# Low parts of the split tokens in the up products: a negated copy and an adding transfer instead of a subtraction

## The chip, the cores and the metric

The kernel runs on one core of one Trainium2 chip. The metric is the device time of one execution in microseconds. The kernel before was timed in three runs: 2589.78, 2593.25 and 2595.57 us, median 2593.25 us.

## The reference, cut to what matters

A hybrid decoder of two layers is stepped once, for a prompt of 1024 tokens and for 8 sample tokens, which the kernel treats together as 1032 tokens of width 1024. The whole is in float32.

```python
def hybrid_layer(x, ...):
    n = rms_norm(x, g_mix)
    z = jnp.einsum('bsd,de->bse', n, w_in)          # q | k | v | conformer input
    ...                                              # dilated attention, causal convolution
    h = x + jnp.einsum('bse,ed->bsd', jnp.concatenate([att, cv], axis=-1), w_o)
    n2 = rms_norm(h, g_ffn)
    f = jnp.square(jax.nn.relu(jnp.einsum('bsd,df->bsf', n2, w_up)))   # 1024 -> 4096
    y = h + jnp.einsum('bsf,fd->bsd', f, w_down)                       # 4096 -> 1024
    return y, new_kv, new_conv
```

The change concerns the product of n2 with w_up, once in each layer.

## The kernel before, in words

Tokens lie along the free dimension, features on the 128 partitions. The normalised activations of the MLP are eight tiles x[0] to x[7], each 128 x 1032. The token axis is cut into two halves of TH = 516.

**Exact products from rounded operands.** TensorE takes operands of type fp32r. To keep the accuracy of float32, each operand is split in two: a high part `h`, which is the value copied by ScalarE to an fp32r tile, and a low part `lo`, the rest, which is the value minus `h`. A product is then three matmuls: weight high by token high, weight high by token low, weight low by token high (lines 966 to 968). Weights are split by `split_piece` (ScalarE line 195, VectorE line 196), tokens of the up products by `split_tokens` (ScalarE line 901, VectorE line 902) and, for the operand t2, by lines 915 and 916.

**Seven products in place of eight.** Both MLP products use a Strassen-like scheme with blocks of 2 x 2. With four k-tiles each, b11 is the first token half of x[0..3], b12 their second half, b21 the first half of x[4..7], b22 their second half. The token operands of the seven products are b21, b11, t2 = b22 - (b12 - b11), t1 = b12 - b11, t3 = b22 - b12, b22 and t4 = b21 - t2. The sums are formed by VectorE in place: b11 is overwritten by t1 (line 909), b12 by t3 (line 921), b21 by t4 (line 918). t2 needs a staging tile of 128 x 1032 for each half of its k-tiles (line 914). The staging tile comes from the pool tag "big", which has three buffers; x[6] and x[7] hold two of them. So the second t2 tile needs the buffer of the first.

The products run in the order a12*b21, a11*b11, s2*t2, s1*t1, s3*t3, s4*b22, a22*t4 (`PRODUCTS`), for each of eight groups of 512 hidden features. `group` loads the weight blocks, forms the weight sums s1 to s4 (line 944), splits them, multiplies and drains. The first product is drained by ScalarE into a new tile f11 (line 995), the second is added into f11 by VectorE (line 991). f11 comes from the pool tag "act", which has six buffers, and in the first group these hold x[0] to x[5]. So the first drain needs an x tile that nobody reads any more. The third product accumulates in the PSUM bank that line 991 reads, and the fourth needs the bank that line 995 reads. The finished hidden tiles are stored to DRAM by GpSimd's queue (line 1017).

**Where the change sits.** Before the up products, `ffn_norm` normalises the output of w_o in two token halves. For each half it stores x to DRAM by GpSimd's queue (line 275), squares it on ScalarE (line 280, into one of two buffers of the tag "out"), adds up the squares on VectorE (line 281), sums over partitions on TensorE (line 306), forms the reciprocal root (line 312 on VectorE, 313 on ScalarE, then three Newton steps, lines 288 to 290), broadcasts it by TensorE (line 319) and ScalarE (line 320) and multiplies (line 284). While the second half is normalised, the first half is already split into b21 and b11.

**What sets the order.** The instructions of each engine run in a fixed order. It is decided when the program is built: a planner models the timeline and lets each engine take, among the instructions whose operands and buffers are ready in its model, the one of highest priority. Priority is program order, except in `later(...)`, which moves a block: loads, sums and splits of the up weights are placed 420 instructions earlier. Waits between engines are put in by the builder, and a buffer is handed on when all its readers are done.

Of the kernel before, what the change touches and what calls it, by code (L numbers as in the profile page):

```python
# [7 lines left out]
F32 = mybir.dt.float32  # L8
F32R = mybir.dt.float32r
AF = mybir.ActivationFunctionType  # L10
ALU = mybir.AluOpType
# [63 lines left out]
def tile_hybrid_decoder_step(  # L75
# [20 lines left out]
    nc = tc.nc  # L96
# [119 lines left out]
    for l in range(DEPTH):  # L216
        for b in range(NB):
            for kv in range(2):
                for g, (win, _) in enumerate(GROUPS):
                    n = (win - 1) * 256  # L220
                    src = caches[g][l, b, kv].rearrange("t h d -> (t h d)")
# [4 lines left out]
                    for q in range(parts):  # L226
                        o = q * rows * step
# [4 lines left out]
    def prow(l, what, j):  # L232
        base = {"mix": 0, "ffn": 8, "cb": 16, "lg": 22, "lb": 28}[what]
        return prm[:, NC_L * l + base + j:NC_L * l + base + j + 1]

    def big(name, dt=F32):
        return tp.tile([P, TOK], dt, tag="big", name=name, bufs=3)
# [9 lines left out]
    def norm_split(xk, gcol, nm, by_chunks=False):  # L247

        xh, xl, acc = [], [], None
        for k in range(KD):  # L250
            x = xk(k)
            h = xs.tile([P, TOK], F32R, tag="xh", name=f"xh{nm}_{k}", bufs=8)
            lo = xs.tile([P, TOK], F32R, tag="xl", name=f"xl{nm}_{k}", bufs=8)
            for a, b in ((0, CHUNKS[1][0]), (CHUNKS[1][0], TOK)) if k == 0 and by_chunks else ((0, TOK),):
                nc.scalar.activation(h[:, a:b], x[:, a:b], AF.Copy, scale=gcol(k))
                nc.vector.scalar_tensor_tensor(lo[:, a:b], x[:, a:b], gcol(k), h[:, a:b].bitcast(F32), op0=ALU.mult, op1=ALU.subtract)  # L256
            xh.append(h)
            xl.append(lo)
            if acc is None:
                acc = tp.tile([P, TOK], F32, tag="acc", name=f"acc{nm}", bufs=1)  # L260
            with later(NORM_LATER):
                if k == 0:
                    nc.scalar.activation(acc, x, AF.Square)
                else:
                    sq = spare(f"sq{nm}_{k}")
                    nc.scalar.activation(sq, x, AF.Square)
                    if k < KD - 1:
                        nc.vector.tensor_tensor(acc, acc, sq, op=ALU.add)
        return xh, xl, acc, sq
# [60 lines left out]
    def layer(l, x_first, x_dram, xin, x_last):  # L330
# [540 lines left out]
        with ExitStack() as pb:  # L871
# [11 lines left out]
            def parts_of(op, name):  # L883

                out = []
                for i in range(2):
                    if op in ("b21", "b11", "t2", "t1"):
                        hl = [xs.tile([P, TOK], F32R, tag=t, name=f"{op}{t}{name}{i}", bufs=8) for t in ("xh", "xl")]
                    else:
                        hl = [bp.tile([P, TOK], F32R, tag=t, name=f"{op}{t}{name}{i}", bufs=6) for t in ("oh", "ol")]  # L890
                    out.append(tuple(t.rearrange("p (k t) -> p k t", k=2) for t in hl))
                return out


            ops = {}

            def split_tokens(op, src):
                o = ops[op] = parts_of(op, f"U{nm}")
                for i in range(4):
                    h, lo_t = (t[:, i % 2, :] for t in o[i // 2])  # L900
                    nc.scalar.activation(h, src(i), AF.Copy)
                    nc.vector.tensor_tensor(lo_t, src(i), h.bitcast(F32), op=ALU.subtract)

            b11, b12 = (lambda i: x[i][:, 0:TH]), (lambda i: x[i][:, TH:])
            b21, b22 = (lambda i: x[4 + i][:, 0:TH]), (lambda i: x[4 + i][:, TH:])
            split_tokens("b21", b21)
            split_tokens("b11", b11)
            for i in range(4):
                nc.vector.tensor_tensor(b11(i), b12(i), b11(i), op=ALU.subtract)
            o = ops["t2"] = parts_of("t2", f"U{nm}")  # L910
            for i in range(2):
                t2 = big(f"t2{nm}_{i}").rearrange("p (k t) -> p k t", k=2)
                for j in range(2):
                    nc.vector.tensor_tensor(t2[:, j, :], b22(2 * i + j), b11(2 * i + j), op=ALU.subtract)
                nc.scalar.activation(o[i][0], t2, AF.Copy)
                nc.vector.tensor_tensor(o[i][1], t2, o[i][0].bitcast(F32), op=ALU.subtract)
                for j in range(2):
                    nc.vector.tensor_tensor(b21(2 * i + j), b21(2 * i + j), t2[:, j, :], op=ALU.subtract)
            split_tokens("t1", b11)
            for i in range(4):  # L920
                nc.vector.tensor_tensor(b12(i), b22(i), b12(i), op=ALU.subtract)
# [103 lines left out]
            for c in range(NG // 2):  # L1025
                ops.clear()
                for _, op in PRODUCTS:
                    o = ops[op] = parts_of(op, f"D{nm}_{c}")
                    for i in range(2):
                        h, lo_t = o[i]  # L1030
# [85 lines left out]
    h, lo, acc, sq = norm_split(first, lambda k: prow(0, "mix", k), "m0", True)  # L1116
# [23 lines left out]
    for l in range(DEPTH):  # L1140
        src = (lambda k: xT[:, k, :]) if l == 0 else (lambda k: x_scr[:, k, :])
        xin = layer(l, None, src, xin, between(l) if l < DEPTH - 1 else finish)
# [102 lines left out]
```

## Time and profile before

| | us |
|---|---|
| median of the three runs | 2593.25 |
| the profiled execution | 2595.12 |
| its span, first to last instruction | 2593.3 |
| TensorE (PE) busy | 2477.9 (96%) |
| VectorE (DVE) busy | 1919.5 (74%) |
| ScalarE (ACT) busy | 1080.7 (42%) |
| GpSimd (POOL) busy | 251.3 (10%) |

The mean granted TensorE clock of the execution is 0.977 of full speed. In a timeline row the first number is the start in us from the beginning of the span, the second how long the instruction, or the run of equal instructions that are shown merged (x3, x4), lasted. Then come engine, line, operation, the tile written and the tiles read, with layer marks such as L and U cut to letters (b21xhUL is the high part of b21 in the up products, b21xlUL its low part; oh and ol are the same for t3, b22 and t4). Square brackets hold the idle time of that engine just before and what ended it.

### The profile page before, as it was taken

To read this page: it belongs to the slowest core of one execution; us is meant where nothing else is said; L and a number is where in the kernel's file an instruction comes from. 1 tells how busy PE (TensorE), PEld (TensorE's weight loads), DVE (VectorE), ACT (ScalarE), POOL (GpSimd) and SP (SyncE) were. 2 spreads that over 40 slices of the span, in tenths; PEclk is the share of its full clock that TensorE was granted. 3 is DMA by queue.
4 is the path that set the end of the run, shared out by engine and by line. 5 is a ranking of instruction groups with operands and counts; after the bars stand their busy time and mean duration, and the time that the engine had idled before them with its cause. 6 is when DMAs were issued, how large, how long until landed. Compare 5 with 4: busy or idle time off the path is not lost.

```text
span 2593.3 us, 47122 instructions
## 1 busy us (share of the span) xinstructions
PE 2477.9 (96%) x18680; PEld 2340.5 (90%) x18680; DVE 1919.5 (74%) x3368; ACT 1080.7 (42%) x2043; POOL 251.3 (10%) x453
## 2 busy tenths in 40 slices
PE   8999999995999999999899999999959999999996
PEld 8988888895999999999898888888859999999996
DVE  7978976669666587778668688756786667886775
ACT  5244448434333353334422444484333333443333
POOL 1001101010001021000010010011101011110001
PEclk9999999997999999999899999999979999999998
DMA  5324423451455587555323252353415555955441
GB/s 183 100 74 115 120 83 113 134 169 70 157 206 194 174 312 252 164 170 204 126 72 106 82 124 74 98 168 100 165 55 186 193 190 184 348 197 196 140 175 66
DMA packets 151374, 391.60 MB, mean 151 GB/s; under 512 B 32033, under 2 KB 51601, under 8 KB 148593
## 3 DMA queue, kind: packets, MB, share of 16 engines
q1 hardware_dynamic: 89632, 210.72, 25.0%
q0 software_dynamic: 43904, 147.95, 16.5%
q10 hardware_dynamic: 17616, 29.91, 3.5%
q8 instruction: 147, 2.41, 0.4%
q14 instruction: 75, 0.61, 0.1%
HBM read 299.38 MB, written 177.06 MB: 184 GB/s over the span
## 4 chain that ended last, share of the span: by engine, by line
PE 73%; issue 11%; DVE 8%; DMA 2%; POOL 1%; ACT 1%; ACTq 0%; DVEq 0%; POOLq 0%; SPq 0%
PE zkL L211 4%; PE zkL L212 4%; PE paDL L966 4%; PE paDL L968 4%; PE zkL L213 4%; PE paDL L967 4%; PE paUL L966 3%; PE paUL L968 3%; PE paUL L967 3%; PE gluL L211 3%; PE sL L573 2%; PE gluL L212 2%; PE gluL L213 2%; PE woL L211 2%; PE woL L212 2%
## 5 line engine op out<-in xcount | busy, mean ns | idle before, releaser
L211 PE MATMUL gluL<-xhm,whi 128*128 128x384 f32 (+1 forms) x576 | 186.9, 330 | 8.4 <-ACT whi L195 5.7
L211 PE MATMUL zkL<-xhm,whi 128*128 128x512 f32 (+2 forms) x576 | 188.6, 327 | 4.4 <-ACT zkL L440 4.4
L212 PE MATMUL zkL<-xlm,whi 128*128 128x512 f32 (+2 forms) x576 | 188.2, 327 | 0.0
L212 PE MATMUL gluL<-xlm,whi 128*128 128x384 f32 (+1 forms) x576 | 187.0, 325 | 0.2 <-DVE xlm L256 0.2
L213 PE MATMUL zkL<-xhm,wlo 128*128 128x512 f32 (+2 forms) x576 | 186.6, 324 | 0.0
L213 PE MATMUL gluL<-xhm,wlo 128*128 128x384 f32 (+1 forms) x576 | 185.8, 325 | 0.0
L385 DVE SCALAR_TENSOR_TENSOR cL<-bxL,hsum,cL 128x512 f32<-128x512 f32 x180 | 134.8, 749 | 0.3
L385 DVE SCALAR_TENSOR_TENSOR cL<-uL,cwt,cL 128x512 f32<-128x512 f32 x180 | 134.4, 752 | 0.0
L212 PE MATMUL woL<-clL,whi 128*128 128x384 f32 (+2 forms) x416 | 130.6, 315 | 0.0
L195 ACT ACTIVATE whi<-raw 128x512 fp32r<-128x512 f32 x152 | 94.1, 634 | 86.4 <-DMA raw<-in_dram 40.1
L211 PE MATMUL woL<-chL,whi 128*128 128x384 f32 (+2 forms) x416 | 129.3, 316 | 0.0
L213 PE MATMUL woL<-chL,wlo 128*128 128x384 f32 (+2 forms) x416 | 128.8, 314 | 0.0
L385 DVE SCALAR_TENSOR_TENSOR bxL<-uL,cwt,bxL 128x512 f32<-128x512 f32 x168 | 126.1, 751 | 0.0
L196 DVE TENSOR_TENSOR wlo<-raw,whi 128x512 fp32r<-128x512 f32 x152 | 103.1, 689 | 31.0 <-ACT whi L195 22.2
L211 PEld LDWEIGHTS zkL<-xhm,whi 128*128 128x128 f32 x576 | 108.4, 188 | 19.0 <-ACT zkL L440 7.0
L211 PEld LDWEIGHTS gluL<-xhm,whi 128*128 128x128 f32 x576 | 109.3, 191 | 12.7 <-ACT whi L195 5.7
L212 PEld LDWEIGHTS zkL<-xlm,whi 128*128 128x128 f32 x576 | 108.6, 189 | 12.2 <-issue 4.7
L213 PEld LDWEIGHTS zkL<-xhm,wlo 128*128 128x128 f32 x576 | 108.6, 188 | 10.7 <-issue 3.2
L212 PEld LDWEIGHTS gluL<-xlm,whi 128*128 128x128 f32 x576 | 109.3, 190 | 2.6 <-issue 1.3
L213 PEld LDWEIGHTS gluL<-xhm,wlo 128*128 128x128 f32 x576 | 109.2, 190 | 1.0 <-DVE wlo L196 0.2
L1038 DVE TENSOR_TENSOR yL<-yL,paDL 128x516 f32<-128x516 f32 x128 | 87.8, 690 | 28.7 <-PE paDL L968 28.5
L585 ACT ACTIVATE smL<-smL,statL 128x128 f32<-128x128 f32 (+1 forms) x192 | 84.6, 443 | 28.4 <-DVE statL L582 27.7
(437 smaller groups left out, 9133.6 us busy)
## 6 DMA issues: line engine op xcount, KB each, us to landing
raw<-in_dram SPq DMA_DIRECT2D x408, 256.0 KB
out_kvs_dram<-in_dram SPq DMA_DIRECT2D x128, 511.8 KB
out_kvs_dram<-in_dram SPq DMA_DIRECT2D x32, 511.0 KB
x_scr<-xL POOLq DMA_DIRECT2D x32, 258.0 KB, 2.4
fdL<-f11L POOLq DMA_DIRECT2D x16, 516.0 KB, 3.2
fdL<-f22L POOLq DMA_DIRECT2D x16, 516.0 KB, 2.9
fdL<-t3fL POOLq DMA_DIRECT2D x16, 516.0 KB, 3.5
fdL<-f12L POOLq DMA_DIRECT2D x16, 516.0 KB, 4.3
```

Of the source, the lines that this page charges most:

```text
L195: nc.scalar.activation(hi, raw, AF.Copy)
L196: nc.vector.tensor_tensor(lo, raw, hi.bitcast(F32), op=ALU.subtract)
L211: nc.tensor.matmul(out[:, :n], a, h, start=(k == 0), stop=False)
L212: nc.tensor.matmul(out[:, :n], a, l, start=False, stop=False)
L213: nc.tensor.matmul(out[:, :n], b, h, start=False, stop=(k == nk - 1))
L385: nc.vector.scalar_tensor_tensor(dst, src(m), tap(m), dst, op0=ALU.mult, op1=ALU.add)
L573: nc.tensor.matmul(sh[h][:, i, :P * len(blocks)], qT[half][hs, n - 4 * half, :], kT[hs, blocks[0]:n + 1, :].rearrange("p b t -> p (b t)"), ...
L585: nc.scalar.activation(sm[:, h, :w], sm[:, h, :w], AF.Exp, bias=stat[g][:, n, c:c + 1], scale=-1.0, accum_out=stat[g][:, n, 4 + c:5 + c])
L966: nc.tensor.matmul(o, wh, h, start=first and k == 0, stop=False, skip_group_check=True)
L967: nc.tensor.matmul(o, wh, lo_t, start=False, stop=False, skip_group_check=True)
L968: nc.tensor.matmul(o, wl, h, start=False, stop=last and k == 3, skip_group_check=True)
L1038: nc.vector.tensor_tensor(o, o, p, op=ALU.add)
```

## The change

The subtraction that forms a low part leaves VectorE in two places: in `split_tokens` (five operands of four tiles in each layer) and for t2 (two tiles of double width in each layer). In its place `rest` first writes the high part times -1 into the low part's tile, on ScalarE, and then issues a transfer from SBUF to SBUF on GpSimd's queue, which adds the source to what lies there. The value that results is the same: source minus high part.

```diff
+            def rest(lo_t, h, src):
+
+                nc.scalar.activation(lo_t, h.bitcast(F32), AF.Copy, scale=-1.0)
+                nc.gpsimd.dma_start(lo_t.bitcast(F32), src, accum_op=ALU.add)
+
             def split_tokens(op, src):
                 o = ops[op] = parts_of(op, f"U{nm}")
                 for i in range(4):
                     h, lo_t = (t[:, i % 2, :] for t in o[i // 2])
                     nc.scalar.activation(h, src(i), AF.Copy)
-                    nc.vector.tensor_tensor(lo_t, src(i), h.bitcast(F32), op=ALU.subtract)
+                    rest(lo_t, h, src(i))
...
                 nc.scalar.activation(o[i][0], t2, AF.Copy)
-                nc.vector.tensor_tensor(o[i][1], t2, o[i][0].bitcast(F32), op=ALU.subtract)
+                rest(o[i][1], o[i][0], t2)
```

The splits of weights, of the tokens of the other products and of the down products stay as they are.

## Rows read from the trace of the kernel before

**Rows 1.** The page, part 1: busy us, share of the span, instructions.
```profile
PE 2477.9 (96%) x18680; PEld 2340.5 (90%) x18680; DVE 1919.5 (74%) x3368; ACT 1080.7 (42%) x2043; POOL 251.3 (10%) x453
```
**Rows 2.** PE timeline, layer 0: start us, us, engine, line, out<-in, [idle before <-releaser].
```profile
604.13 0.66 PE L306 MATMUL rsfL<-accfL,ones 128*32 128x64 f32 x16 [9.70 <-DVE accfL L281]
...
614.75 0.58 PE L966 MATMUL pdUL<-b21xhUL,whia12UL 128*128 128x258 f32 x1 [0.48 <-ACT accfL L320]
...
641.51 0.58 PE L966 MATMUL paUL<-t2xhUL,whis2UL 128*128 128x258 f32 x1 [13.22 <-DVE f11L L991]
```
**Rows 3.** PE timeline, layer 1, end of the second gap.
```profile
1924.10 0.80 PE L966 MATMUL pbUL<-t1xhUL,whis1UL 128*128 128x258 f32 x2 [15.03 <-ACT t1xhUL L901]
```
**Rows 4.** DVE timeline, layer 0, first gap.
```profile
600.26 0.69 DVE L281 TENSOR_TENSOR accfL<-accfL,sqfL 128x516 f32<-128x516 f32 x1
600.87 1.91 DVE L902 TENSOR_TENSOR b21xlUL<-xL,b21xhUL 128x516 fp32r<-128x516 f32 x3
602.69 0.69 DVE L902 TENSOR_TENSOR b11xlUL<-xL,b11xhUL 128x516 fp32r<-128x516 f32 x1
603.29 0.69 DVE L281 TENSOR_TENSOR accfL<-accfL,sqfL 128x516 f32<-128x516 f32 x1
603.90 1.91 DVE L902 TENSOR_TENSOR b11xlUL<-xL,b11xhUL 128x516 fp32r<-128x516 f32 x3
...
606.32 0.29 DVE L312 TENSOR_SCALAR rqfL<-rsfL 128x129 f32<-128x129 f32 x1
```
**Rows 5.** ACT timeline, layer 0, second gap.
```profile
628.75 0.62 ACT L901 ACTIVATE t3ohUL<-xL 128x516 fp32r<-128x516 f32 x1
629.27 1.05 ACT L915 ACTIVATE t2xhUL<-t2L 128x1032 fp32r<-128x1032 f32 x1
...
631.27 2.19 ACT L901 ACTIVATE b22ohUL<-xL 128x516 fp32r<-128x516 f32 x4
...
639.07 1.09 ACT L995 ACTIVATE f11L<-pdUL 128x516 f32<-128x516 f32 x2 [4.04 <-DVE t4olUL L902]
640.89 1.06 ACT L915 ACTIVATE t2xhUL<-t2L 128x1032 fp32r<-128x1032 f32 x1 [0.72 <-DVE t2L L914]
641.86 2.19 ACT L901 ACTIVATE t1xhUL<-xL 128x516 fp32r<-128x516 f32 x4
643.96 1.14 ACT L901 ACTIVATE t4ohUL<-xL 128x516 fp32r<-128x516 f32 x2
```
**Rows 6.** DVE timeline, layer 0, end of the second gap.
```profile
638.32 1.32 DVE L902 TENSOR_TENSOR t4olUL<-xL,t4ohUL 128x516 fp32r<-128x516 f32 x2
639.53 1.32 DVE L914 TENSOR_TENSOR t2L<-xL,xL 128x516 f32<-128x516 f32 x2
640.74 1.32 DVE L991 TENSOR_TENSOR f11L<-f11L,paUL 128x516 f32<-128x516 f32 x2
```
**Rows 7.** DVE timeline, layer 1, first gap.
```profile
1880.97 0.69 DVE L281 TENSOR_TENSOR accfL<-accfL,sqfL 128x516 f32<-128x516 f32 x1
...
1884.00 0.70 DVE L281 TENSOR_TENSOR accfL<-accfL,sqfL 128x516 f32<-128x516 f32 x1
...
1887.03 0.70 DVE L281 TENSOR_TENSOR accfL<-accfL,sqfL 128x516 f32<-128x516 f32 x1
```
**Rows 8.** ACT timeline, first gap of layer 0 and of layer 1.
```profile
598.38 1.97 ACT L901 ACTIVATE b21xhUL<-xL 128x516 fp32r<-128x516 f32 x3 [2.48 <-DVE xL L284]
...
1883.58 0.62 ACT L280 ACTIVATE sqfL<-xL 128x516 f32<-128x516 f32 x1
```
**Rows 9.** The page, part 6: issues, KB each, median us to landing.
```profile
x_scr<-xL POOLq DMA_DIRECT2D x32, 258.0 KB, 2.4
fdL<-f11L POOLq DMA_DIRECT2D x16, 516.0 KB, 3.2
```
**Rows 10.** POOL timeline, layer 0: one issue.
```profile
593.18 0.54 POOL L275 DMA_DIRECT2D x_scr<-xL  x1 [0.73 <-DVE xL L850]
```
**Rows 11.** ACT timeline, layer 1, start of the second gap.
```profile
1909.81 0.63 ACT L901 ACTIVATE t3ohUL<-xL 128x516 fp32r<-128x516 f32 x1 [0.89 <-DVE xL L921]
```

## The prediction

> **What bounds the kernel now.** I read the page's engine list first: TensorE is busy for nearly the whole span [rows 1]. So only the few stretches in which it stands still can be won or lost. A list of PE's waits shows the two longest of each layer where the MLP begins, the place of the edit, and the PE timeline dates them. In layer 0 PE waits 9.70 us for the sum of squares of the second token half (first gap), works on the rest of that norm until the first product at 614.75, computes two products, and stands still again for 13.22 us until 641.51 (second gap) [rows 2]. Layer 1 has the same pair; its second gap is 15.0 us and ends at 1924.10 [rows 3].
>
> Then I read the timelines of VectorE (DVE) and ScalarE (ACT) inside the gaps. In the first gap DVE works through normalisation, rests ("lo", L902) and the last two squares' additions in one queue. The addition that PE waits for starts at 603.29, behind four rests; L312, which needs only PE's short sum, starts at 606.32, behind four more [rows 4]. In the second gap the end is set by the drain of the first product. ACT's copy f11 (L995) waits 4.04 us for the rest t4 [rows 5], because f11 takes the buffer of an x tile and t4 is that tile's last reader. Only then can DVE add the second product into f11 (L991, 640.74 [rows 6]) and PE go on. So both gaps lie on DVE's queue, and the change takes work out of it: a gain was to be expected. The question is what ACT and the transfers do with it.
>
> **The change part by part.** Per layer 20 rests of 128x516 and two of 128x1032 leave DVE; as many ACT copies by -1 come in, each followed by a transfer of GpSimd's queue that adds the source.
>
> *First gap, DVE's side.* Three rests in a row take 1.91 us, the next starts 1.82 us after the first: 0.61 us a place in the queue [rows 4]. Layer 0: the addition at 600.26 is followed at once by the one now at 603.29, so that one starts near 600.87, lasts 0.69 and ends at 601.56. PE then needs 0.66 us with some 0.1 us of handover (603.98 to 604.13) on either side [rows 2], so L312 starts near 602.4 in place of 606.32. That is 3.9 us earlier; what follows L312 (the Newton steps, the broadcast on PE, the first product) keeps its order and moves with it. Layer 1: three additions stand at 1880.97, 1884.00 and 1887.03 [rows 7]. The last one's square on ACT (1883.58 [rows 8]) can only begin once the addition of 1880.97 gives up its buffer, at 1881.67. I allow 0.3 us for an ACT instruction under way, 0.62 for the square and 0.1 of handover: the last addition starts near 1882.65 in place of 1887.03, 4.4 us earlier. Sum: -8.3 us.
>
> *First gap, what ACT and the transfers need.* ACT starts the splits at 598.38 [rows 8] and has 16 in place of 8, at 2.19/4 = 0.547 us each [rows 5]: done near 607.2, with the root (L313) in between near 607.6. A 258 KB transfer from SBUF issued by GpSimd lands 2.4 us after issue [rows 9], and issue takes 0.54 us on POOL [rows 10], less than the 1.1 us in which ACT makes one h and one -h. So the last rest is there near 610, and the first product, now at 614.75 - 3.9 = 610.85, finds it. The margin is under 1 us. L909 overwrites b11 and must now wait until the transfers have read it; it runs some 8 us after them. I cost both at nothing; if the cover fails, at 1 us each.
>
> *Second gap.* Here the same move turns against the kernel. I keep the clock of the old trace and subtract the 3.9 and 4.4 us at the end. From 628.75, when ACT takes the first t3 split [rows 5], its list to the end of the splits is: t3, b22, t4 and t1 with four tiles each, h and -h, 32 x 0.547 = 17.5 us; t2 twice, h and -h, 4 x 1.05 = 4.2 us [rows 5]. Together 21.7 us, half of it new. In the old trace ACT ran dry after the first t4 copies, because t2's second half and t1 weren't ready, and so took f11 as soon as DVE freed its buffer; then came t2, t1 and the rest of t4 [rows 5]. Will ACT run dry in the changed kernel? The second t2 needs the staging buffer of the first. That is given up when its transfer has landed: t2 h and -h end near 631.4, a 516 KB transfer takes 3.2 us [rows 9], so near 634.6. DVE, no longer full of rests, forms the second t2 in 1.32 us [rows 6]: 635.9. By then ACT has done the 8 for t3 and one or two for b22 and is still full. So t2, t1, b22 and t4, which all stand ahead of the drain in the program, reach ACT without a pause, and f11 comes last: 628.75 + 21.7 = 650.45. Its first half takes 0.6 us, which frees the bank for PE: 651.05 in place of 641.51, +9.5 us. Layer 1: ACT's list starts at 1909.81 [rows 11], ends at 1931.5; PE at 1932.1 in place of 1924.10, +8.0 us. Sum: +17.5 us. Everything PE multiplies after that has landed by then, so no further wait follows.
>
> On GpSimd's queue only later transfers and the first fd store stand behind a transfer that waits for ACT; the store is due after PE's restart.
>
> *Transfers.* No row shows a transfer that adds. Nearest rows: from 258 KB to 516 KB the time goes from 2.4 to 3.2 us [rows 9], 0.8 us per 258 KB, under the 1.1 us at which ACT supplies them: no cost. Upper end: nothing overlaps and each 258 KB holds the queue for its whole 2.4 us. I take the lower, since these rows show the same queue reading the same memory.
>
> The Trainium skill ("DMA: Bandwidth & Descriptors", section "Rules for kernel authors") says that an accumulating transfer reads its destination and writes it later, so it carries a third stream; by that the 0.8 us would be an estimated 1.2 us, the transfers would fall slightly behind ACT, and the sum would be some 1 to 2 us higher. No run here shows it; it speaks for the slow-transfer rival below.
>
> *Sum.* -8.3 + 17.5 = +9.2 us. The profiled execution took 2595.12 us (span 2593.3), 1.9 us above the median 2593.25; on the median this gives 2602.5 us.
>
> **The rivals.**
> *The drain goes early (faster).* Should the order on ACT put f11 in as soon as an x tile is free, the price of the second gap nearly vanishes. Earliest tile: t1's first, whose -h comes after t3 (8), the first two of b22, t2 (4 x 1.05): 628.75 + 12 x 0.547 + 4.2 = 639.5, landing at 641.9, f11 done at 642.5, +1.0 us in layer 0; by the same 13.75 us 1923.6 in layer 1, -0.5. Sum -8.3 + 0.5 = -7.8: 2585.5 us. For it: in the old order the drain did stand ahead of t2, t1 and the late t4. Against it: that was while these were not ready.
> *The drain falls in the middle.* If it comes after t1 and b22 but before t4 is through, it runs near 646.1: +5.2 and +3.7 us, in sum +0.6: 2593.9 us, no change. This needs a pause in ACT's list that I don't see.
> *The adding transfers are slow (slower still).* At 2.4 us per 258 KB one after the other, the t2, t3, b22, t2, t1 transfers up to t1's first take about 24 us from 631.4: 655.4, and no x tile is free before. With the copy PE restarts near 656, 5 us later per layer than forecast: +19 us, 2612.5. It decides from about 2.2 us of queue time per 258 KB; beyond that the first gap suffers as well. Against it: the rows above.
>
> **How the numbers follow.** Forecast 0.52; early drain 0.23; middle 0.11; slow transfers 0.14. A measurement here tells about 0.2%, 5.2 us. Forecast lies within 2598 to 2608: mostly slower, 0.08 of it within 5.2 us. Early drain: 0.20 faster, 0.03 same. Middle: 0.09 same, 0.02 slower. That gives faster 0.20, same 0.20, slower 0.60. The range leaves out about half of the early drain and of the slow transfers: 2586 to 2618; the forecast's own range is 2598 to 2608.
>
> **What would show it.** DVE: no L902 or L916, the last addition right behind L284, L312 near 602.4. First product near 611 and 1893. ACT: h and -h in pairs, 22 more instructions per layer, no pause before f11, and f11 behind the t1 and t4 copies. PE's second gap near 23 us in both layers, released by f11 or L991. Transfers of 258 KB landing in some 2.4 us. Wrong if f11 stands ahead of t1 on ACT, if the PE wait ends on a transfer, or if the first gap is not shorter by 3 us or more.

## The result, and the profile after

The changed kernel took 2624.07 us (median of four runs, 2621.75 to 2624.83) against 2592.81 us for the kernel before in the same session: a ratio of 1.0119, 95% interval 1.0102 to 1.0137. It is slower, as forecast, but by some 31 us where 9 were forecast; it lies outside the range of 2586 to 2618. The profiled execution took 2624.44 us (span 2622.7). In the changed kernel the line numbers behind the edit are five higher: the copies by -1 are L899, the adding transfers L900, the high parts L906 and L920, t2's subtraction L919, the products L971 to L973, the drain f11 L1000. In the kernels of the experiments they differ by a few more; there the tile names tell the instructions apart.

The page's engine list of the changed kernel, to be laid beside [rows 1]:

```profile
PE 2480.2 (95%) x18680; PEld 2341.7 (89%) x18680; DVE 1885.4 (72%) x3316; ACT 1108.5 (42%) x2095; POOL 296.6 (11%) x505
```

VectorE lost 34 us of work and ScalarE gained 28, which is what was meant. The counts set one number right: 52 instructions left VectorE, and 52 came to ScalarE and to GpSimd's queue, 26 per layer. `split_tokens` runs for six operands (b21, b11, t1, t3, b22, t4), so there are 24 rests and the two of t2 in a layer, where the section on the change and the prediction count 20 and two, and the text on e1 below counts 44 transfers in all. The prediction's times don't hang on this, since its lists name the operands of each gap rightly. TensorE has the same work, so the loss is standstill. The list of PE's waits of the changed kernel (releaser, total us, times, longest) says where:

```profile
PE pbUL L971 <- ACT f11L L1000: 46.2, 2, 23.5
PE rsfL L306 <- DVE accfL L281: 18.6, 2, 11.2
PE pbUL L972 <- DMA t1xlUL<-xL: 9.6, 2, 4.8
```

The waits of the first gap (rsfL) are 3.7 us shorter in total; they were 9.70 us [rows 2] and, in layer 1, 12.60. The second gap grew from 13.2 + 15.0 [rows 2, 3] to 46.2 us, and behind it stands a wait that the kernel before has not: for the transfers that finish t1's low part. The PE timeline of the changed kernel, layer 0 and then layer 1:

```profile
601.59 0.66 PE L306 MATMUL rsfL<-accfL,ones 128*32 128x64 f32 x16 [7.37 <-DVE accfL L281]
...
611.98 0.58 PE L971 MATMUL pdUL<-b21xhUL,whia12UL 128*128 128x258 f32 x1 [0.48 <-ACT accfL L320]
...
615.69 0.58 PE L972 MATMUL pdUL<-b21xlUL,whia12UL 128*128 128x258 f32 x1 [1.19 <-DMA b21xlUL<-xL]
...
650.68 0.58 PE L971 MATMUL pbUL<-t1xhUL,whis1UL 128*128 128x258 f32 x1 [22.74 <-ACT f11L L1000]
...
656.03 0.58 PE L972 MATMUL pbUL<-t1xlUL,whis1UL 128*128 128x258 f32 x1 [4.77 <-DMA t1xlUL<-xL]
...
1948.93 0.58 PE L971 MATMUL pbUL<-t1xhUL,whis1UL 128*128 128x258 f32 x1 [23.48 <-ACT f11L L1000]
...
1954.33 0.58 PE L972 MATMUL pbUL<-t1xlUL,whis1UL 128*128 128x258 f32 x1 [4.82 <-DMA t1xlUL<-xL]
```

**A ruler for the stage.** Work elsewhere drifts by a few us between profiled executions. So I measure each layer's stage by itself: from the start of the first b21 split on ACT to the second group's first f11 copy on ACT. In layer 0 of the kernel before that is 675.44 - 598.38 = 77.06 us, in the changed kernel 689.73 - 598.17 = 91.56. These are the rows of both layers; the first split of the kernel before in layer 0 stands in [rows 8].

```profile
675.44 0.60 ACT L995 ACTIVATE f11L<-pdUL 128x516 f32<-128x516 f32 x1 [0.76 <-PE pdUL L968]
...
1879.09 1.97 ACT L901 ACTIVATE b21xhUL<-xL 128x516 fp32r<-128x516 f32 x3 [2.45 <-DVE xL L284]
...
1958.41 0.60 ACT L995 ACTIVATE f11L<-pdUL 128x516 f32<-128x516 f32 x1 [0.76 <-PE pdUL L968]
```
```profile
598.17 1.30 ACT L906 ACTIVATE b21xhUL<-xL 128x516 fp32r<-128x516 f32 x2 [2.48 <-DVE xL L284]
...
689.73 0.60 ACT L1000 ACTIVATE f11L<-pdUL 128x516 f32<-128x516 f32 x1 [0.64 <-PE pdUL L973]
...
1895.65 1.30 ACT L906 ACTIVATE b21xhUL<-xL 128x516 fp32r<-128x516 f32 x2 [2.45 <-DVE xL L284]
...
1987.53 0.60 ACT L1000 ACTIVATE f11L<-pdUL 128x516 f32<-128x516 f32 x1 [0.77 <-PE pdUL L973]
```

So layer 0 costs 14.5 us more, and layer 1, measured alike, 12.6 (91.88 against 79.32). That is 27.1 of the 29.3 us between the two profiled executions. The other 2.3 us lie outside the stage, where the two programs do the same work; they are not explained. The profiled executions of all fourteen kernels took 2434.8 to 2439.7 us outside the stage (span less stage), in no order that follows the changes, so differences of this size there can't be read.

### The profile page after: what moved, and what is told of

Its sections match the earlier page's. It is cut to its first block, busy times and chain, and to the rows that moved or that the text cites. A ratio compares the mean times of both kernels' runs of the same rounds, so it can differ in the third digit from the quotient of the medians.

```text
span 2622.7 us, 47284 instructions
## 1 busy us (share of the span) xinstructions
PE 2480.2 (95%) x18680; PEld 2341.7 (89%) x18680; DVE 1885.4 (72%) x3316; ACT 1108.5 (42%) x2095; POOL 296.6 (11%) x505
## 3 DMA queue, kind: packets, MB, share of 16 engines
q10 hardware_dynamic: 17616, 29.91, 3.4%
## 4 chain that ended last, share of the span: by engine, by line
PE 73%; issue 13%; DVE 6%; DMA 2%; POOL 2%; ACT 1%; ACTq 0%; DVEq 0%; POOLq 0%
PE paDL L971 4%; PE paDL L973 4%; PE paDL L972 4%; PE zkL L211 4%; PE zkL L212 4%; PE zkL L213 4%; PE gluL L211 3%; PE sL L573 3%; PE gluL L212 3%; PE gluL L213 3%; PE woL L211 2%; PE woL L212 2%; PE woL L213 2%; PE paUL L971 2%; PE paUL L973 2%
## 5 line engine op out<-in xcount | busy, mean ns | idle before, releaser
L213 PEld LDWEIGHTS zkL<-xhm,wlo 128*128 128x128 f32 x576 | 108.6, 188 | 10.7 <-issue 3.2
L971 PE MATMUL pbUL<-t1xhUL,whis1UL 128*128 128x258 f32 x256 | 73.1, 287 | 46.2 <-ACT f11L L1000 46.2
```

The source lines that it names most:

```text
L213: nc.tensor.matmul(out[:, :n], b, h, start=False, stop=(k == nk - 1))
L971: nc.tensor.matmul(o, wh, h, start=first and k == 0, stop=False, skip_group_check=True)
```

## The experiments

Ratios are against the kernel before on the same chip. "Stage" is the sum over both layers by the ruler above, against the kernel before's 156.4 us, from one profiled execution each.

| kernel | median us | ratio (95%) | stage, us |
|---|---|---|---|
| the change | 2624.07 | 1.0119 (1.0102-1.0137) | +27.1 |
| e3 first gap alone | 2593.98 | 0.9997 (0.9987-1.0007) | -0.2 |
| e4 second gap alone | 2627.28 | 1.0126 (1.0111-1.0141) | +30.8 |
| e1 transfers copy, don't add | 2609.24 | 1.0056 (1.0041-1.0071) | +11.9 |
| e2 VectorE adds, no transfers | 2605.55 | 1.0045 (1.0030-1.0060) | +12.6 |
| e8 change, f11 in its own buffer | 2618.43 | 1.0093 (1.0079-1.0107) | +25.4 |
| e5 GpSimd subtracts b21, b11 | 2600.57 | 1.0027 (1.0015-1.0039) | +5.8 |
| e12 e5, own buffer, t1 first | 2603.96 | 1.0038 (1.0025-1.0051) | +6.5 |
| e15 before, own buffer, t1 first | 2595.95 | 1.0007 (0.9999-1.0016) | +0.5 |
| e9 before, own buffer | 2597.77 | 1.0011 (1.0002-1.0020) | +3.0 |
| e17 b22 alone the new way | 2593.53 | 0.9995 (0.9987-1.0004) | -2.2 |
| e18 b22 and t3 the new way | 2598.03 | 1.0013 (1.0004-1.0022) | +4.5 |
| e16 e18 with own buffer | 2588.03 | 0.9975 (0.9967-0.9984) | -6.5 |

**Which half costs: e3 and e4.** Only some operands go the new way, the rest stay on VectorE (in e3 b21 and b11, in e4 all others).

```diff
-                    rest(lo_t, h, src(i))
+                    if op in ("b21", "b11"):          # e4: ("t1", "t3", "b22", "t4"), and t2
+                        rest(lo_t, h, src(i))
+                    else:
+                        nc.vector.tensor_tensor(lo_t, src(i), h.bitcast(F32), op=ALU.subtract)
```

> Only b21 and b11, the operands split in the first gap, take the new way; t1, t2, t3, t4 and b22 keep VectorE's subtraction. Theory A: what the shorter queue of VectorE gains (2.8 us in layer 0, 1.5 us in layer 1 to the first product) is about lost again to the late b21 transfer in layer 0: 2588 to 2593 us. Forecast's first step (minus 8.3 us): 2584.5 us. Rival D (the transfers of the first gap cause a good part of the loss): 2598 us or more.

> Only t1, t2, t3, t4 and b22 take the new way; b21 and b11 keep VectorE's subtraction. Theory A: the whole loss is here, 14 us a layer: 2618 to 2625 us. Rival D: 2605 to 2612 us.

The whole loss is in the second gap: e4 took 2627.28 us, a little more than the 2618 to 2625 expected. The first gap gives no gain at all: e3 took 2593.98 us, where 2588 to 2593 were expected. (In the stage the two add up to 3.5 us more than the change; this is not explained.) Why not is read from the stretch of the first two products, whose 96 matmuls the windows view shows (start:end, length, busy PE, PEld, DVE, ACT and POOL with instruction counts, granted clock, DMA share, GB/s). In order: the kernel before, the changed one, e3 and e1, layer 0.

```profile
614.75:628.29 13.54, 13.54 (x96) 13.34 (x96) 13.54 (x23) 2.61 (x5) 0.00 (x0) 0.85 0.24 79
```
```profile
611.98:627.94 15.96, 14.77 (x96) 14.27 (x96) 15.38 (x26) 2.61 (x5) 0.00 (x0) 0.77 0.37 97
```
```profile
611.84:628.67 16.83, 15.65 (x96) 15.15 (x96) 15.57 (x26) 2.61 (x5) 0.00 (x0) 0.72 0.35 92
```
```profile
610.28:623.48 13.20, 13.19 (x96) 12.99 (x96) 13.20 (x22) 2.62 (x5) 0.00 (x0) 0.88 0.24 81
```

With adding transfers the first product starts 2.6 us earlier (13.8 us after the first split in place of 16.4), but the two products take 2.4 to 3.3 us longer: PE stops 1.2 us for b21's last low part, and the granted clock stays at 0.77 and 0.72 in place of 0.85. After its standstill PE runs at the lower of its two levels (0.42 us per matmul in place of 0.28); in the kernel before it reaches the full one 3.8 us after the first product, in the changed kernel and e3, with the stop in between, after 7.3 and 9.2 us, in e1, without a stop, after 3.0. Two rows of the changed kernel, on either side of the rise:

```profile
619.08 0.42 PE L972 MATMUL pdUL<-b21xlUL,whia12UL 128*128 128x258 f32 x1
...
619.62 0.28 PE L972 MATMUL pdUL<-b21xlUL,whia12UL 128*128 128x258 f32 x1
```

The rise scatters between executions. Over both layers of all kernels here it came 2.3 to 5.1 us after the first product where PE did not stop, and 7.3 to 9.2 us after it in the three cases with the stop (layer 0 of the changed kernel, of e3 and of e8).

**Which ingredient costs: e1 and e2.** e1 lets the transfer copy where it added, and so leaves out the subtraction; the order on every engine is that of the changed kernel. e2 keeps ScalarE's copies by -1 and adds on VectorE.

```diff
-                nc.gpsimd.dma_start(lo_t.bitcast(F32), src, accum_op=ALU.add)
+                nc.gpsimd.dma_start(lo_t.bitcast(F32), src)                                      # e1
+                nc.vector.tensor_tensor(lo_t, src, lo_t.bitcast(F32), op=ALU.add)                # e2
```

> The changed kernel, but each of the 44 transfers copies the source over the low part instead of adding it (the low part is then the whole value, so the products are not the reference's). The order of every engine is that of the changed kernel. Theory A (the adding itself is slow: 190 GB/s against 413 GB/s of the plain store, so the queue falls behind ScalarE): the wait for t1's low part (4.8 us a layer), the wait for b21's (1.2 us and the longer half-speed stretch after it, some 2.4 us in layer 0) and the last wait of the drain for t4 (0.9 to 1.0 us a layer) go; 8 to 15 us less than the changed kernel, 2609 to 2616 us. Rival B (any transfer between two tiles of SBUF over GpSimd's queue is as slow): no difference, 2624 us within 3.

> No transfers: ScalarE still writes minus the high part, and VectorE adds the source, so VectorE has its old load and ScalarE the new one. Theory A: ScalarE's doubled list is itself worth a good half of the loss, since the first drain stays near the end of it: 5 to 8 us a layer, 2603 to 2609 us, first drain on ScalarE near 647 in layer 0. Rival C (the loss lies in the transfers alone, ScalarE has room): 2593 us within 3.

Both came out as the theory expected (2609 to 2616, and 2603 to 2609), and the rivals, 2624 for e1 and 2593 for e2, fell. e1 recovers half of the loss: some 15 us are the price of adding in the transfer. The DMA view of the second gap shows it, first the changed kernel (630 to 664 us), then e1 (628 to 650): GB/s in 40 equal slices (for the changed kernel also the busy share of the DMA engines in tenths), and for t4 and t1 the count, KB each and median us to landing.

```profile
DMA  0790999999999999999999999999999999999941
GB/s 5 226 694 5 172 228 192 214 172 194 163 187 185 177 182 180 189 180 194 180 187 192 172 189 204 170 177 189 185 192 189 189 194 192 192 194 267 301 194 73
...
t4olUL<-xL POOLq DMA_DIRECT2D x4, 258.0 KB, 10.8
t1xlUL<-xL POOLq DMA_DIRECT2D x4, 258.0 KB, 10.6
```
```profile
GB/s 138 134 347 902 238 0 53 383 398 338 323 270 375 233 323 368 315 353 405 353 53 0 0 293 188 0 38 413 398 270 375 383 368 308 368 398 368 158 315 405
...
t4olUL<-xL POOLq DMA_DIRECT2D x4, 258.0 KB, 3.8
t1xlUL<-xL POOLq DMA_DIRECT2D x4, 258.0 KB, 3.6
```

In the changed kernel the sixteen DMA engines were 90% busy or more in every slice of nearly all of that stretch, at about 190 GB/s, without a pause; e1's slices show pauses (0, 38, 53) and between them mostly 300 to 410. At 190 GB/s the 264,192 bytes of one transfer take 1.39 us, and ScalarE supplies one in 1.1 us: the queue falls behind from transfer to transfer, and the t1 and t4 transfers land after more than 10 us. What in the adding costs is not shown. By the pages (part 3, queue q0) the 52 adding transfers went in 7488 packets, e1's copies of the same bytes in 4416, so that the adding and the finer cut come together here. In e1 the wait for t1's low part is gone and f11 waits for nothing. What is left of e1's loss, 11.9 us in the stage, goes back to ScalarE's list: its second gaps, 21.62 and 21.63 us, are together 15.0 longer than before and end on f11 at the end of that list, and 3.1 us come back in the first gap. e2, with no transfer at all, loses as much (12.6), of which 10.7 lie in the second gaps; there the planner put f11 ahead of three t1 copies, and the second gap of layer 0 still took 19.0 us:

```profile
647.05 1.06 ACT L1000 ACTIVATE f11L<-pdUL 128x516 f32<-128x516 f32 x2
```
```profile
647.68 1.07 PE L971 MATMUL pbUL<-t1xhUL,whis1UL 128*128 128x258 f32 x2 [19.02 <-ACT f11L L1000]
```

**Is it f11's place in the list: e8, e9, e15.** f11 of the first group gets the free buffer of tag "acc", so that it needs no x tile. e8 is the changed kernel with this, e9 the kernel before with this, e15 the kernel before with this and with t1's splits moved ahead of t2's.

```diff
+                            own = g == 0 and n == "f11"
-                            c[n] = tp.tile([P, TOK], F32, tag="act", name=f"{n}{nm}_{g}", bufs=NCT)
+                            c[n] = tp.tile([P, TOK], F32, tag="acc" if own else "act", name=f"{n}{nm}_{g}", bufs=1 if own else NCT)
...
+            split_tokens("t1", b11)                    # e15, e12
             o = ops["t2"] = parts_of("t2", f"U{nm}")
...
-            split_tokens("t1", b11)                    # e15, e12
```

> The changed kernel, but the first drain f11 of the first group gets the buffer of the norm's sums, which is free by then, in place of an x tile's. So the drain no longer waits for ScalarE's list or for a transfer. Theory A: little is won, because t2's second half and t1 still hang on ScalarE's list and on the slow adding transfers; PE resumes when t2's second low part lands near 653 in layer 0: 2614 to 2622 us. Rival E (the drain's late place is the cause by itself): 2603 to 2609 us.

> The kernel before with f11 of the first group in a buffer of its own and nothing else; every low part is subtracted on VectorE. The kernel with the own buffer and the adding transfers for b22 and t3 took 0.9975 of before. Theory (the gain needs both: the own buffer takes the drain off the x tiles, the eight rests off VectorE bring t2's second half): this one gains less, 2590 to 2595 us, PE waiting for t2's second half on VectorE. Rival (the own buffer does it all): 2585 to 2589 us.

> The kernel before with only the drain's buffer and the order of t1 changed; all low parts by VectorE. Theory A: s1*t1 (some 6 us at full clock) moves into the second gap, while t2's second half comes some 2.5 us later: 4 to 6 us a layer less, 2581 to 2586 us. If VectorE's queue as a whole sets the restart: 2590 to 2595 us.

e8 came out as expected (2614 to 2622); its rival, that the place of f11 is most of the loss (2603 to 2609), fell. The early drain moves the wait. By the medians it saves some 7 us of 31, but in the stage only 1.7 of 27.1; the rest lies outside, where such differences can't be read. What an early drain is worth beside ScalarE's longer list alone, without adding transfers, no run shows. PE now takes t2 first, and stops twice for its low part, which adding transfers finish:

```profile
641.43 0.58 PE L972 MATMUL paUL<-t2xlUL,whis2UL 128*128 128x258 f32 x1 [9.45 <-DMA t2xlUL<-t2L]
...
657.57 0.58 PE L972 MATMUL paUL<-t2xlUL,whis2UL 128*128 128x258 f32 x1 [12.29 <-DMA t2xlUL<-t2L]
```

In e9 and e15 the drain is early too, and nothing is gained: e15 was expected at 2581 to 2586 and took 2595.95 us, e9 at 2590 to 2595 and took 2597.77; the rival that e9 does it all, 2585 to 2589, fell. The cause is the next wait: t2's second half, which VectorE forms behind its queue of rests. In e9 it comes at 642.39, and ACT and PE wait for it; e15 stands still for it all the same (7.05 us), after s1*t1.

```profile
642.39 1.30 DVE L914 TENSOR_TENSOR t2L<-xL,xL 128x516 f32<-128x516 f32 x2
```
```profile
644.83 0.80 PE L966 MATMUL paUL<-t2xhUL,whis2UL 128*128 128x258 f32 x2 [6.39 <-ACT t2xhUL L915]
```

**GpSimd itself subtracts: e5 and e12.** In the kernel before, `nc.gpsimd.tensor_tensor` forms b21's and b11's low parts; e12 adds the buffer and the t1 order of e15.

```diff
-                    nc.vector.tensor_tensor(lo_t, src(i), h.bitcast(F32), op=ALU.subtract)
+                    eng = nc.gpsimd if op in ("b21", "b11") else nc.vector
+                    eng.tensor_tensor(lo_t, src(i), h.bitcast(F32), op=ALU.subtract)
```

> The kernel before, with the low parts of b21 and b11 subtracted by GpSimd itself (one instruction each, 1.53 us as the final norm's products on GpSimd show), no extra ScalarE work and no transfer. Theory A (the first gap's gain was real and was spent on ScalarE's longer list and the late transfer): the forecast's first step appears, 6 to 8 us less than before, 2585 to 2588 us, first product near 611 in layer 0. Rival F (the first gap is set by something that moves along, no gain to be had): 2592 to 2595 us.

> A candidate for a faster kernel: the kernel before, with GpSimd subtracting for b21 and b11, the first drain in the free buffer, and t1 split ahead of t2, so that PE can do s1*t1 while t2 is formed. If both gaps are read rightly, 6 to 8 us from the first gap and 4 to 6 us a layer from the second: 2574 to 2580 us. If the second gap is bound by VectorE's queue as a whole, only the first part: 2586 us.

Expected were 2585 to 2588 us for e5, and 2574 to 2580 for e12; both missed and are slower than before. While GpSimd's subtractions run, VectorE's instructions with two inputs from SBUF stretch. The timelines of e5, POOL first, then DVE:

```profile
598.25 6.38 POOL L903 TENSOR_TENSOR b21xlUL<-xL,b21xhUL 128x516 fp32r<-128x516 f32 x3 [5.37 <-ACT b21xhUL L901]
604.60 6.35 POOL L903 TENSOR_TENSOR b11xlUL<-xL,b11xhUL 128x516 fp32r<-128x516 f32 x4
```
```profile
602.60 0.29 DVE L312 TENSOR_SCALAR rqfL<-rsfL 128x129 f32<-128x129 f32 x1 [0.78 <-PE rsfL L306]
...
605.11 1.35 DVE L288 SCALAR_TENSOR_TENSOR rqfL<-rqfL 128x129 f32<-128x129 f32 x1
...
609.74 1.35 DVE L289 TENSOR_TENSOR rqfL<-rqfL 128x129 f32<-128x129 f32 x1
```

L288 and L289 take 1.35 us; in the changed kernel (below) L288 takes 0.29. L312, whose only tile input is the sum that PE left in PSUM, keeps its 0.29 us beside GpSimd. The Newton steps stand on the path to the first product, and so the offload loses there more than it saves: in layer 0 PE's sum came 1.4 us earlier after the first split than in the kernel before, its broadcast 3.5 us later. The Trainium skill ("SBUF — State Buffer", section "Who interferes with whom") says that VectorE shares its second SBUF port pair with GpSimd under an exclusive lock, and that a VectorE instruction with two SBUF inputs contends with a GpSimd instruction that reads SBUF; these rows agree (1.35 us in place of 0.29 with two SBUF inputs, 0.29 for L312 with none). In e3, where transfers took the place of GpSimd's arithmetic, L288 kept 0.29 us.

**How much may go the new way: e17, e18, e16.** The late operands only: b22 in e17, b22 and t3 in e18, and e18 with f11's own buffer in e16 (diffs as in e3 and e8).

> Only the four low parts of b22 (per layer) go the new way; all others are subtracted on VectorE as before. Theory (the loss of the change is a matter of amount: ACT has about 4 us idle ahead of f11 in the second gap, and b22 is needed late): VectorE's queue ahead of t4 loses 4 x 0.61 = 2.4 us, ACT's gains 4 x 0.547 = 2.2 us inside its idle time, the adding transfers land long before product 6 reads them; both second gaps 2.4 us shorter, about 2587 to 2591 us against 2593. Rival (any order of the rests ends at the same restart, since t2's second half on VectorE and ACT sets it): 2592 to 2596. If adding transfers hurt by themselves (memory or queue contention): above 2597.

> The low parts of b22 and of t3 go the new way (eight transfers per layer), the others are subtracted on VectorE as before. Theory (a matter of amount): VectorE's queue ahead of t4 loses 8 x 0.61 = 4.9 us, ACT's gains 8 x 0.547 = 4.4 us against 4.0 us of idle time, so f11 can come 3 to 4 us earlier: 2585 to 2590 us. Rival (the restart is set by t2's second half or by ACT's list, which is now full): 2592 to 2598. The transfers hold no x tile that f11 needs, since t4 and t1 stay on VectorE, so no f11 wait on a transfer.

> As the kernel with the low parts of b22 and t3 the new way, and f11 of the first group in a buffer of its own, so that it waits for no x tile. Theory: f11 then runs as soon as the first product is done, and PE restarts when t2's high part is there, whose second half stands behind eight rests fewer on VectorE (4.9 us): both second gaps 3 to 5 us shorter than in the kernel before, 2583 to 2588 us. Rival (t3's and b22's copies stand ahead of t2's on ACT and take back what VectorE gains): 2591 to 2597.

In e17 and e18 the rivals were right (e18 at the upper edge of 2592 to 2598): e17 is no change that can be told, and e18 shows the list again. Its drain:

```profile
645.07 1.06 ACT L1003 ACTIVATE f11L<-pdUL 128x516 f32<-128x516 f32 x2
```

ScalarE's pause ahead of f11 is used up, and f11 goes behind t4's copies, 45.2 us after the first split (645.07 - 599.84) in place of 40.7 (639.07 - 598.38 [rows 5, 8]). e16 takes it out of that list; it came out where its theory put it, at the edge (2583 to 2588), and is faster than both kernels. PE's second gap there falls apart into four short waits:

```profile
629.99 0.35 PE L974 MATMUL paUL<-t2xhUL,whis2UL 128*128 128x258 f32 x1 [2.24 <-DVE f11L L1000]
...
632.32 0.58 PE L974 MATMUL paUL<-t2xhUL,whis2UL 128*128 128x258 f32 x1 [1.97 <-DVE f11L L1000]
...
634.67 0.58 PE L975 MATMUL paUL<-t2xlUL,whis2UL 128*128 128x258 f32 x1 [1.77 <-DVE t2xlUL L924]
...
639.68 0.80 PE L974 MATMUL paUL<-t2xhUL,whis2UL 128*128 128x258 f32 x2 [2.49 <-ACT t2xhUL L923]
```

t2's second half is formed at 635.67, 37.5 us after the first split, in e9 43.5 us after it, since eight rests have left VectorE's queue. The b22 and t3 transfers still land late in layer 0, after 7.3 and 4.8 us, but PE reads them only in the sixth and fifth product. Neither part does it alone: the buffer alone gives 1.0011, the eight transfers alone 1.0013, both together 0.9975.

## Why the prediction was wrong: which steps held and which failed

**The ScalarE list in the second gap: held.** Forecast was a list of 21.7 us without a pause, the drain last, PE restarting at 651.05 and 1932.1 on the clock of the old trace, +9.5 and +8.0 us. The ACT timeline of the changed kernel:

```profile
628.40 0.62 ACT L906 ACTIVATE t3ohUL<-xL 128x516 fp32r<-128x516 f32 x1
...
647.89 1.14 ACT L899 ACTIVATE t4olUL<-t4ohUL 128x516 fp32r<-128x516 f32 x2
650.03 1.09 ACT L1000 ACTIVATE f11L<-pdUL 128x516 f32<-128x516 f32 x2 [1.00 <-DMA t4olUL<-xL]
```

From 628.40 to 650.03 are 21.6 us, of which 20.6 are the list and 1.0 a wait for a transfer that the forecast had not (0.9 in layer 1). PE's own second gap is 22.74 - 13.22 = 9.5 us longer in layer 0, and 23.48 - 15.03 = 8.5 in layer 1: 18.0 against the forecast 17.5, and 16.1 without the two waits. So the mechanism held, and that the size came so near is in part luck: the list was some 1 us shorter than forecast, and the wait for the transfer made up for it. e2 confirms the mechanism without any transfer. The early-drain rival fell; e8 shows that even an early drain would not have made its 2585 us.

**"Transfers": failed; this is the first mis-sized term.** The prediction bounded an adding transfer between 0.8 us and 2.4 us per 258 KB, took the lower end from plain stores and wrote "no cost". Measured: 1.39 us, over the 1.1 us of ScalarE's supply. The claim that "Everything PE multiplies after that has landed by then" fell with it: t1's low part came 4.77 and 4.82 us late, 9.6 us together. The slow-transfer rival named the mechanism, but let it decide only "from about 2.2 us" and act on f11 through the x tiles. It decided earlier and mainly elsewhere: at PE's wait for t1's low part, whose transfers are issued near the end and so have nearly the whole queue ahead of them. The rival's own sum was also too small: at 2.4 us per 258 KB the transfers that it names (three or four of t3, four of b22, the two of t2 with 516 KB each, the first of t1) take 29 to 31 us and not 24, so that its 2612.5 should have been about 2622 to 2627 us. That the measured 2624.07 lies there is luck, since the transfers took 1.39 us and not 2.4. Of the 15.2 us of the stage that e1 gets back, these waits make 9.6, those ahead of f11 1.9, and 2.8 are in layer 0's first gap, at whose end the second one begins 27.0 us after the first split in e1; 0.9 are not traced. The rule of the Trainium skill that the prediction weighed ("DMA: Bandwidth & Descriptors", "Rules for kernel authors": the accumulate reads its destination and writes it later) pointed the right way; the estimate of 1.2 us that the prediction worked out with it lies nearer to the measured 1.39 than the 0.8 taken.

**The first gap, -8.3 us: failed; the second mis-sized term.** It came to -0.3. Counted from the first split on ACT, the second gap begins at 29.77 us where it began at 29.91 in layer 0 (598.17 to 650.68 - 22.74; 598.38 to 641.51 - 13.22), and at 29.80 where it began at 29.98 in layer 1. Three things took the 8.3 us. The timelines of the changed kernel, DVE in both layers, then ACT in layer 0:

```profile
600.05 1.49 DVE L281 TENSOR_TENSOR accfL<-accfL,sqfL 128x516 f32<-128x516 f32 x2
602.32 0.29 DVE L312 TENSOR_SCALAR rqfL<-rsfL 128x129 f32<-128x129 f32 x1 [0.78 <-PE rsfL L306]
...
606.03 0.29 DVE L288 SCALAR_TENSOR_TENSOR rqfL<-rqfL 128x129 f32<-128x129 f32 x1 [1.01 <-ACT rqfL L313]
...
1902.21 0.70 DVE L281 TENSOR_TENSOR accfL<-accfL,sqfL 128x516 f32<-128x516 f32 x1 [3.19 <-ACT sqfL L280]
```
```profile
604.08 1.66 ACT L899 ACTIVATE b11xlUL<-b11xhUL 128x516 fp32r<-128x516 f32 x3
605.65 0.35 ACT L313 ACTIVATE rqfL<-rsfL,eps 128x129 f32<-128x129 f32 x1
605.90 0.62 ACT L899 ACTIVATE b11xlUL<-b11xhUL 128x516 fp32r<-128x516 f32 x1
606.42 0.62 ACT L899 ACTIVATE b21xlUL<-b21xhUL 128x516 fp32r<-128x516 f32 x1
```

- The last addition stands right behind and L312 at 602.32, as forecast (602.4). But the root L313 now waits behind copies by -1 on ScalarE until 605.65. That "what follows L312 ... keeps its order and moves with it" was wrong: counted from the first split, 2.6 us of the 3.9 reached the first product.
- In layer 1 the last square stands on ScalarE behind the copy under way and six more (four of b11, one of b21, one by -1). The forecast gave 0.3 us for "an ACT instruction under way"; DVE waited 3.19 us for the square, and by the ruler's start 1.4 us were gained where 4.4 were forecast.
- b21's last low part, "near 610" in the forecast with a margin under 1 us, came when PE had already stopped for it, at 615.69. ScalarE had written its copy in time (606.42, the last of its list); the adding transfer, issued behind the others, was late, so this is the first mis-sized term again. The stop took 1.2 us, and the clock that stayed low longer (0.77 against 0.85) about as much. In layer 1 PE did not stop, and the two products still took 14.05 us in place of 12.85, at a clock of 0.82 against 0.90; that took 1.2 of the 1.4 us gained. e1's layer 1, without adding, took 14.06, so the adding is not the reason; since the rise scatters between executions, it is not shown that the change is. The prediction had priced the cover's failure at 1 us and the clock not at all.

**The sum.** -8.3 became -0.32, +17.5 became +17.97, and 0 became +9.59: together 27.2, beside 27.1 measured for the stage.

## What to carry to other kernels

Work taken from a busy engine on the path is worth only what the next one in line leaves: here ScalarE's list took VectorE's place in both gaps, and an order that had a pause for the drain lost it. Price a new kind of transfer by its rate against the rate of its supplier, take that rate from a transfer of the same kind (here a plain store's 0.8 us stood in for 1.39), and look at the consumer of the last one in the queue. Moving only what is read late (b22, t3), and freeing the drain from the buffers of the moved readers at the same time, turned the same idea into a gain of 0.25%.

## What the runs showed of the hardware

- A transfer from SBUF to SBUF that adds ran at about 190 GB/s with the sixteen DMA engines 90% busy or more throughout; the same transfers as plain copies ran mostly at 300 to 410 (e1). Its issue on POOL took 0.83 to 2.51 us in the changed kernel, against 0.54 for e1's copies and for a plain store [rows 10].
- GpSimd's subtraction of 128x516 took 6.35/4 = 1.59 us, and slowed VectorE's two-input instructions beside it: from 0.29 to 1.35 us for 128x129 (e5).
- After the first gap TensorE reached its higher level 2.3 to 5.1 us after the first product, and 7.3 to 9.2 us after it in the three cases in which it stopped again for a transfer in between.
